# Zero products ahead of the state and join products of a chunked recurrence

## The chip, the cores and the metric

The program runs on one NeuronCore of one Trainium2 chip. The metric is the device time of one execution in microseconds. Of the kernel before there are three timed runs and one profiled execution.

## What is computed

One inference step of two decoder layers for a prompt of 1024 tokens and eight samples. Layer 0 is a convolution branch beside a sparse-attention branch. Layer 1 is RWKV-7 time mixing, and only this layer's recurrence is touched. For each of 16 heads with a 64 x 64 state S it is, token by token:

```
sa = S kk_t
S  = S * w_t - sa (kk_t * a_t)^T + v_t k_t^T
y_t = S r_t
```

Before it stand the projections r, k, v, z and two small hidden layers for w and a, behind it a norm over each head, a gate and an output projection.

## The kernel before

`phase_d` computes layer 1. The recurrence is done in chunks of 64 tokens. A **unit** is a pair (g, d): 128 tokens (two chunks c = 0, 1) of half of the heads, so there are 16 units. Four generators serve a unit:

- `s1` loads the unit's rows and makes its factors, with products into `sm` and `pa` (L1361 to L1431);
- `s2` inverts small triangular blocks on VectorE;
- `joinUT` joins the blocks into the 64 x 64 inverse `UT`. It has four join steps, each a burst of tiny products into the one bank `pg`: L1488 and L1496 with 64 products each, L1511 and L1519 with 16 each. A first step writes `pg`, ScalarE copies it to `Gs` (L1490), the second step multiplies `Gs` into a new `pg`, that is copied into `UT`, and the last two steps do the same again (copies L1514 and L1522);
- `s3` carries the state. Per chunk it multiplies the state into half 0 of the bank `pA` (the first state step, `pA<-SV,AM`, L1541), copies this to `E` on VectorE (L1549), multiplies `UT` by `E` into half 1 of `pA` (the second state step, `pA<-E,UT`), copies it to `SV` (L1560, L1561), and accumulates the new state and the outputs in `pB`.

Beside the units runs the **background**: the projections of the second half of the prompt, z, and the output projections (`t_proj`, `t_sigma`, `t_a`, `t_out`), with products of 256 or 512 columns (L1195 to L1197, L1245 to L1248, L1807 to L1809). The list `F1` holds it. For every unit the loop makes eight turns; a turn takes one step of `s3`, in turns 4 to 7 one join step of the next unit, a step of `s2` of the next unit, one of `s1` of the unit after it, and then about one step of the background.

That loop is the order in which the instructions are traced. The order on each engine's queue is set by a scheduler that simulates the program: what it takes to be ready goes first, and what is traced earlier has precedence. So a state product can be queued ahead of background that was traced before it. An instruction given to `keep_in_program_order` is queued behind the instruction of its engine that was traced last before it. TensorE takes its queue's products in order.

In the last unit (7, 1) `warm` already puts four zero products into a `pg` bank behind each of the six steps of `s3` (L1531), 24 in all.

The `pg`, `pA` and `pB` banks exist once each.

Of the kernel before, what the change touches and what calls it, by code (L numbers as in the profile page):

```python
# [10 lines left out]
BF = mybir.dt.bfloat16  # L11
# [1098 lines left out]
def phase_d(nc, tc, I, O, G):  # L1110
# [4 lines left out]
    flat = lambda t: t.rearrange("p a b -> p (a b)")  # L1115
    with ExitStack() as es:
# [3 lines left out]
        late = pool("dl", 1)  # L1120
# [321 lines left out]
        def s2(g, d, J):  # L1442
# [31 lines left out]
                nc.sync.dma_start(UT[16 * b:16 * b + 16, :, o:o + 16], ud[b * 8:b * 8 + 8].rearrange("c s t -> s c t"))  # L1474
            yield

        def joinUT(J):
            UT = J.UT
            ABf = J.AB.rearrange("p j c t -> p (j c) t")
            U = up.tile([128, 2, 8, 32], F32, name="U")  # L1480
            for o in range(2):
                nc.vector.transpose(U[:, o], UT[:, :, 32 * o:32 * o + 32])
            pg = pq.tile([128, 8, 32], F32, name="pg")
            Gs = up.tile([128, 8, 32], F32, name="Gs")
            for c in range(8):
                for a in range(0, 128, 32):
                    o = a // 32 % 2
                    nc.tensor.matmul(pg[a:a + 32, c, 0:16], lhsT=ABf[a:a + 16, c, 32 * o:32 * o + 32],  # L1488
                                     rhs=U[a:a + 16, o, c, 0:16], start=True, stop=True)
            nc.scalar.activation(Gs[:, :, 0:16], pg[:, :, 0:16], AF.Copy)  # L1490
            yield
            pt = pq.tile([128, 8, 32], F32, name="pg")
            for c in range(8):
                for a in range(0, 128, 32):
                    o = a % 64
                    nc.tensor.matmul(pt[a:a + 16, c, 0:16], lhsT=Gs[a:a + 32, c, 0:16], rhs=UT[a:a + 32, c, o + 16:o + 32],  # L1496
                                     start=True, stop=True)
            for a in range(0, 128, 32):
                o = a % 64 + 16
                if a % 64:  # L1500
                    nc.vector.tensor_copy(UT[a:a + 16, :, o:o + 16], pt[a:a + 16, :, 0:16])
                else:
                    nc.scalar.activation(UT[a:a + 16, :, o:o + 16], pt[a:a + 16, :, 0:16], AF.Copy)
            U = up.tile([128, 8, 32], F32, name="U")
            nc.vector.transpose(U, UT[:, :, 0:32])
            yield
            pg = pq.tile([128, 8, 32], F32, name="pg")
            Gs = up.tile([128, 8, 32], F32, name="Gs")
            for c in range(8):
                for a in (0, 64):  # L1510
                    nc.tensor.matmul(pg[a + 32:a + 64, c, 0:32], lhsT=ABf[a:a + 32, c, 32:64], rhs=U[a:a + 32, c],  # L1511
                                     start=True, stop=True)
            for a in (0, 64):
                nc.scalar.activation(Gs[a + 32:a + 64], pg[a + 32:a + 64, :, 0:32], AF.Copy)  # L1514
            yield
            pt = pq.tile([128, 8, 32], F32, name="pg")
            for c in range(8):
                for a in (0, 64):
                    nc.tensor.matmul(pt[a:a + 32, c, 0:32], lhsT=Gs[a + 32:a + 64, c], rhs=UT[a + 32:a + 64, c, 32:64],  # L1519
                                     start=True, stop=True)  # L1520
            for a in (0, 64):
                nc.vector.tensor_copy(UT[a:a + 32, :, 32:64], pt[a:a + 32, :, 0:32])  # L1522
            yield

        wz = late.tile([128, 512], BF, name="wz")
        nc.gpsimd.memset(wz, 0.0)

        def warm(n):
            z = pq.tile([128, 8, 32], F32, name="pg")
            for _ in range(n):  # L1530
                tc.keep_in_program_order(nc.tensor.matmul(flat(z), lhsT=wz[:, 0:128], rhs=wz[:, 0:256], start=True, stop=True))  # L1531

        def s3(g, d, J):
            wn = 4 if (g, d) == (7, 1) else 0
            AM, SV, MRB, BK, PC, UT = J.AM, J.SV, J.MRB, J.BK, J.PC, J.UT
            js = slice(4 * d, 4 * d + 4)
            for h, i in HV:
                nc.gpsimd.tensor_copy(SV[h, :, i, 0], ST[h, js])
            Y = up.tile([128, 4, 128], F32, name="Y")
            MH = [(m, h, i) for m in range(4) for h, i in HV]  # L1540
            mm = lambda out, lhsT, rhs, start: nc.tensor.matmul(out, lhsT=lhsT, rhs=rhs, start=start, stop=True,  # L1541
                                                                skip_group_check=True)
            for c in range(2):
                pA = py_.tile([128, 2, 4, 64], F32, name="pA")
                pB = py_.tile([128, 2, 4, 64], F32, name="pB")
                for m, h, i in MH:
                    mm(pA[h, 0, m], AM[:, m, i, c], SV[:, m, i, c], m == 0)
                E = up.tile([128, 4, 64], F32, name="E")
                nc.vector.tensor_copy(E, pA[:, 0])  # L1549
                pc = PC.rearrange("p (m c) -> p m c", c=2)[:, :, c]  # L1550
                for m, h, i in MH:
                    mm(pB[h, 1, m], SV[h, m, i, c], AM[h, m, 2, c], m == 0)
                for h, i in HV:
                    mm(pB[h, 0], ident[h, h], SV[h, :, i, c], False)
                if wn:
                    warm(wn)
                yield
                for m, h, i in MH:
                    mm(pA[h, 1, m], UT[h, 2 * m + c], E[h, m], False)
                nc.scalar.activation(SV[0:64, :, 0, c], pA[0:64, 1], AF.Copy)  # L1560
                nc.vector.tensor_copy(SV[64:128, :, 1, c], pA[64:128, 1])  # L1561
                if wn:
                    warm(wn)
                yield
                for m, h, i in MH:
                    mm(pB[h, 0, m], BK[:, m, c, i], SV[:, m, i, c], False)
                for m, h, i in MH:
                    mm(pB[h, 1, m], SV[:, m, i, c], MRB[:, m, c, i], False)
                for h, i in HV:
                    dst = SV[h, :, i, 1] if c == 0 else ST[h, js]  # L1570
                    nc.vector.tensor_tensor(dst, pB[h, 0], pc[h].unsqueeze(2).to_broadcast([64, 4, 64]), op=MUL)
                nc.scalar.activation(Y[:, :, 64 * c:64 * c + 64], pB[:, 1], AF.Copy)
                if wn:
                    warm(wn)
                yield
            yc = (py_ if YC else pm).tile([128, 512], F32, name="pA" if YC else "sm")
            nc.tensor.matmul(yc, lhsT=K["cent"], rhs=flat(Y), start=True, stop=True)
            ycv = yc.rearrange("p (m t) -> p m t", m=4)
            sq = up.tile([128, 4, 128], F32, name="sq")
            nc.scalar.activation(flat(sq), yc, AF.Square)  # L1580
            for m in range(4):
                nc.scalar.activation(Y[:, m], ycv[:, m], AF.Copy, scale=V(4 * d + m, 3))
            yield
            var = (py_ if YC else pm).tile([128, 512], F32, name="pB" if YC else "sm")
            nc.tensor.matmul(var, lhsT=K["bones"], rhs=flat(sq), start=True, stop=True)
            nc.scalar.activation(flat(sq), var, AF.Ln, scale=1.0 / 64, bias=C["eps_gn"])
            nc.scalar.activation(sq, sq, AF.Exp, scale=-0.5)
            nc.vector.tensor_tensor(sq, Y, sq, op=MUL)
            nc.vector.tensor_tensor(sq, sq, J.bv, op=ADD)
            if TL and (g, d) == (7, 1):  # L1590
                G.Y = sq
            else:
                nc.sync.dma_start(YT[g // 2][d][:, :, g % 2 * 128:g % 2 * 128 + 128], sq)
            yield
# [254 lines left out]
        g1 = [s1(*units[u], JJ[u]) for u in range(16)] + [none, none]  # L1849
        g2 = [s2(*units[u], JJ[u]) for u in range(16)] + [none]  # L1850
        gj = [joinUT(J) for J in JJ] + [none]
        for g in (g1[0], g1[1], g2[0], gj[0]):
            for _ in g:
# [32 lines left out]
def body(tc, I, O, stage="all"):  # L1886
# [4 lines left out]
    with ExitStack() as es:  # L1891
# [34 lines left out]
        if stage == "C":  # L1926
            for q in range(2):
                nc.sync.dma_start(O["d_x1T"][:, :, q * 512:q * 512 + 512], G.scr["x1T"][q][:, :, 0:512])
            return
        phase_d(nc, tc, I, O, G)  # L1930


# [80 lines left out]
```

## Time and profile before

| | |
|---|---|
| median of 3 runs | 2153.94 us (2147.12 to 2162.48) |
| profiled execution, its own time | 2146.61 us |
| its span, first to last instruction | 2144.6 us |
| busy: TensorE products, VectorE, ScalarE, GpSimd | 85%, 69%, 53%, 44% |
| mean granted TensorE clock | 0.889 |

A granted clock of 1.00 is TensorE's upper level, 2.4 GHz, and 0.50 its lower, 1.2 GHz. "Busy" of TensorE is the union of its products' durations, whose ends are modelled. An fp32 product appears as two records, so the 8 products of a state step count as x16 in the rows. Idle time before an instruction is that of its engine, with what ended it.

### The profile page before, as it was taken

How to read it: one execution, taken by the hardware profiler on the slowest of the kernel's cores; microseconds unless marked ns; L12 is line 12 of the kernel's file. 1: busy time of each engine (PE TensorE's matmuls, PEld its weight loads, DVE VectorE, ACT ScalarE, POOL GpSimd, SP SyncE). 2: the span in 40 equal slices, each digit the busy share in tenths (PEclk: the TensorE clock that was granted, in tenths of full speed). 3: DMA queues.
4: the chain of work that ended last, by engine and by line, in shares of the span. 5: the costliest groups of instructions: out<-in, count | busy, mean ns of one | idle time of the engine just before them, and what ended most of it. 6: DMA issues, size and time to landing. Idle time of an engine off the chain costs nothing. (4 is left out here: it accounts for less than half of the span.)

```text
span 2144.6 us, 41476 instructions
## 1 busy us (share of the span) xinstructions
PE 1826.6 (85%) x16106; PEld 1528.2 (71%) x16106; DVE 1474.2 (69%) x2550; ACT 1144.5 (53%) x2353; POOL 934.3 (44%) x765
## 2 busy tenths in 40 slices
PE   5997997848998998798878899899999886999875
PEld 5896886836776786575767898678688754976654
DVE  5998995467887788425645347873855899466864
ACT  3233224555665556356746555865874467455544
POOL 4667676564655455354534421242344435212211
PEclk9898998958998887798889899979789997999778
DMA  6424334440221112545656534443443445443443
GB/s 241 140 71 148 119 121 172 170 146 19 68 63 49 53 54 65 165 129 156 184 190 197 173 117 106 130 133 115 126 146 126 146 144 166 131 112 103 152 148 101
DMA packets 231519, 273.18 MB, mean 127 GB/s; under 512 B 71481, under 2 KB 171505, under 8 KB 227162
## 3 DMA queue, kind: packets, MB, share of 16 engines
q1 hardware_dynamic: 210136, 213.11, 32.5%
q0 software_dynamic: 7616, 41.52, 5.8%
q10 hardware_dynamic: 13570, 15.90, 2.1%
q8 instruction: 127, 2.08, 0.4%
q14 instruction: 70, 0.57, 0.1%
HBM read 210.37 MB, written 64.27 MB: 128 GB/s over the span
## 5 line engine op out<-in xcount | busy, mean ns | idle before, releaser
L121 POOL TENSOR_TENSOR wl<-w,wh 128x1024 fp32r<-128x1024 f32 x76 | 195.5, 2573 | 341.6 <-ACT wh L113 330.3
L1195 PE MATMUL mm<-xh,wh 128*128 128x256 f32 (+1 forms) x1024 | 308.2, 303 | 20.9 <-ACT og L1330 10.9
L1197 PE MATMUL mm<-xh,wl 128*128 128x256 f32 (+1 forms) x1024 | 300.5, 295 | 4.4 <-POOL wl L121 4.4
L1196 PE MATMUL mm<-xl,wh 128*128 128x256 f32 (+1 forms) x1024 | 302.8, 296 | 1.6 <-POOL xk L1215 0.8
L1195 PEld LDWEIGHTS mm<-xh,wh 128*128 128x128 f32 x1024 | 202.6, 199 | 33.4 <-ACT og L1330 13.7
L113 ACT ACTIVATE wh<-w 128x1024 fp32r<-128x1024 f32 (+1 forms) x122 | 126.0, 1034 | 165.5 <-DMA w<-in_w_fm 60.7
L1197 PEld LDWEIGHTS mm<-xh,wl 128*128 128x128 f32 x1024 | 202.9, 199 | 9.5 <-POOL wl L121 5.6
L1196 PEld LDWEIGHTS mm<-xl,wh 128*128 128x128 f32 x1024 | 204.3, 200 | 5.1 <-issue 2.1
L268 DVE SCALAR_TENSOR_TENSOR c<-U,cw,c 128x1024 f32<-128x1024 f32 x120 | 198.0, 1674 | 0.9
L604 POOL TENSOR_TENSOR Pl<-PT,Ph 128x512 fp32r<-128x512 f32 (+1 forms) x102 | 132.1, 1299 | 145.9 <-DVE Ph L603 114.9
L252 POOL TENSOR_TENSOR cbuf<-cbuf 128x256 f32<-128x256 f32 (+2 forms) x72 | 131.1, 1827 | 85.8 <-ACT cbuf L250 82.9
L217 PE MATMUL S<-xh,wh 128*128 128x344 f32 (+1 forms) x432 | 147.1, 341 | 23.3 <-ACT wh L113 19.3
L219 PE MATMUL S<-xh,wl 128*128 128x344 f32 (+1 forms) x432 | 145.6, 337 | 14.6 <-POOL wl L121 11.2
L218 PE MATMUL S<-xl,wh 128*128 128x344 f32 (+1 forms) x432 | 146.7, 340 | 3.8 <-POOL xl L121 3.7
L1223 POOL TENSOR_TENSOR xl<-xs,xh 128x520 fp32r<-128x520 f32 (+1 forms) x76 | 106.5, 1404 | 82.5 <-ACT xh L1222 80.7
L250 ACT ACTIVATE cbuf<-cbuf,wrow 128x256 f32<-128x256 f32 x192 | 79.3, 495 | 113.3 <-DMA cbuf<-in_ccmp,cix 72.1
L1219 DVE SCALAR_TENSOR_TENSOR xs<-xk,mu,xs 128x512 f32<-128x512 f32 x96 | 94.4, 989 | 55.2 <-ACT xs L1218 54.3
L217 PEld LDWEIGHTS S<-xh,wh 128*128 128x128 f32 (+1 forms) x432 | 85.4, 198 | 25.6 <-ACT wh L113 24.1
L562 DVE TENSOR_REDUCE nm<-S 128x1 f32<-128x640 f32 (+7 forms) x128 | 88.2, 698 | 19.8 <-PE S L558 19.0
L219 PEld LDWEIGHTS S<-xh,wl 128*128 128x128 f32 (+1 forms) x432 | 84.9, 197 | 19.7 <-POOL wl L121 13.4
L602 ACT ACTIVATE PT<-mm 128x512 f32<-128x512 f32 (+1 forms) x102 | 59.4, 586 | 57.9 <-PE mm L590 46.8
L218 PEld LDWEIGHTS S<-xl,wh 128*128 128x128 f32 (+1 forms) x432 | 84.9, 196 | 7.0 <-POOL xl L121 4.5
(666 smaller groups left out, 5305.1 us busy)
## 6 DMA issues: line engine op xcount, KB each, us to landing
w<-in_w_rkvz SPq DMA_DIRECT2D x64, 512.0 KB
w<-in_w_out SPq DMA_DIRECT2D x32, 512.0 KB
w<-in_w_fm SPq DMA_DIRECT2D x25, 512.0 KB
xk<-x1T SPq DMA_DIRECT2D x48, 260.0 KB
xk<-x1T SPq DMA_DIRECT2D x48, 256.0 KB
w<-in_w_out SPq DMA_DIRECT2D x16, 256.0 KB
x<-in_xp SPq DMA_DIRECT2D x8, 512.0 KB
x<-x ACTq DMA_DIRECT2D x8, 512.0 KB
```

Of the source, the lines that this page charges most:

```text
L113: nc.scalar.activation(hi, src, AF.Copy, **({} if scale is None else {"scale": scale}))
L121: e_lo.tensor_tensor(lo, src, hi, op=SUB)
L217: nc.tensor.matmul(dst, lhsT=wh[:, k, 0:n], rhs=xh[:, k, sl], start=k == 0, stop=False)
L218: nc.tensor.matmul(dst, lhsT=wh[:, k, 0:n], rhs=xl[:, k, sl], start=False, stop=False)
L219: nc.tensor.matmul(dst, lhsT=wl[:, k, 0:n], rhs=xh[:, k, sl], start=False, stop=k == 7)
L252: nc.gpsimd.tensor_tensor(bv[:, 0:n], bv[:, 0:n], bv[:, n:2 * n], op=ADD)
L268: e.scalar_tensor_tensor(c[:, i, 0:T], u[:, k:k + T], cwh[:, i, k:k + 1], c[:, i, 0:T], op0=MUL, op1=ADD)
L604: lambda: nc.gpsimd.tensor_tensor(Pl[:, 0:w], PT[:, 0:w], Ph[:, 0:w], op=SUB)]
L1195: nc.tensor.matmul(dst, lhsT=wh[:, k], rhs=xh[k][:, lo:hi], start=k == 0, stop=False)
L1196: nc.tensor.matmul(dst, lhsT=wh[:, k], rhs=xl[k][:, lo:hi], start=False, stop=False)
L1197: nc.tensor.matmul(dst, lhsT=wl[:, k], rhs=xh[k][:, lo:hi], start=False, stop=k == 7)
L1223: (nc.vector if early[0] and k % LD == 0 else nc.gpsimd).tensor_tensor(lo[k][:, 0:n], t[:, 0:n], hi[k][:, 0:n], op=SUB)
```

## The change

Two functions get zero products of 128 x 128 by 256 bf16 columns, two at a time, each kept in program order. In `joinUT` they are written into the bank of each of the four join steps before its real products, in `s3` into half 0 of `pA` before the first state step and into half 1 before the second, for both chunks, in all 16 units. The real products that follow overwrite them or add to zeros. The zero tile `wz` is made half as wide and is traced earlier.

```
+        wz = late.tile([128, 256], BF, name="wz")
+        nc.gpsimd.memset(wz, 0.0)
+        def fillw(z, n):
+            for _ in range(n):
+                tc.keep_in_program_order(nc.tensor.matmul(z, lhsT=wz[:, 0:128], rhs=wz, start=True, stop=True,
+                                                          skip_group_check=True))
...
             pg = pq.tile([128, 8, 32], F32, name="pg")
+            fillw(flat(pg), 2)
...
             pt = pq.tile([128, 8, 32], F32, name="pg")
+            fillw(flat(pt), 2)
...
-        wz = late.tile([128, 512], BF, name="wz")
-        nc.gpsimd.memset(wz, 0.0)
...
+                fillw(pA[:, 0].rearrange("p m t -> p (m t)"), 2)
                 for m, h, i in MH:
                     mm(pA[h, 0, m], AM[:, m, i, c], SV[:, m, i, c], m == 0)
...
                 yield
+                fillw(pA[:, 1].rearrange("p m t -> p (m t)"), 2)
                 for m, h, i in MH:
                     mm(pA[h, 1, m], UT[h, 2 * m + c], E[h, m], False)
```

The two `pg` pairs shown stand twice, once for the join of 16-blocks and once for that of 32-blocks.

## Rows read from the trace of the kernel before

**Rows 1.** Windows of the unit loop: length, busy (count) per engine, granted clock, DMA.
```profile
1250.00:1360.00 110.00, 102.92 (x1471) 88.09 (x1469) 80.44 (x159) 72.91 (x163) 24.37 (x30) 1.00 0.43 119
1360.00:1440.00 80.00, 68.61 (x783) 51.77 (x784) 69.06 (x137) 64.83 (x132) 28.55 (x35) 0.79 0.43 125
1440.00:1495.00 55.00, 54.34 (x713) 50.03 (x712) 19.75 (x40) 23.55 (x52) 11.47 (x9) 1.00 0.35 107
1495.00:1580.00 85.00, 75.97 (x924) 60.53 (x925) 69.22 (x134) 68.76 (x153) 36.52 (x44) 0.78 0.46 142
1580.00:1690.00 110.00, 106.51 (x1206) 96.04 (x1206) 63.20 (x113) 58.57 (x118) 44.44 (x32) 1.00 0.46 139
...
1830.00:1905.00 75.00, 74.13 (x1021) 65.40 (x1021) 36.11 (x79) 42.98 (x85) 15.04 (x14) 1.00 0.33 97
...
sum 850.00, PE 754.49 PEld 609.67 DVE 600.93 ACT 518.49 POOL 253.69; mean PE 75.45 PEld 60.97 DVE 60.09 ACT 51.85 POOL 25.37
```
**Rows 2.** Windows of the 18 stretches at half clock between 1250 and 2100.
```profile
1362.00:1365.40 3.40, 3.31 (x33) 2.85 (x35) 1.47 (x3) 3.35 (x5) 0.90 (x1) 0.50 0.42 123
...
2082.20:2089.00 6.80, 6.11 (x52) 2.81 (x46) 1.23 (x4) 4.51 (x9) 0.00 (x0) 0.50 0.09 21
sum 173.90, PE 143.54 PEld 109.04 DVE 139.92 ACT 110.81 POOL 57.09; mean PE 7.97 PEld 6.06 DVE 7.77 ACT 6.16 POOL 3.17
```
**Rows 3.** Windows of the 4 us ahead of each of these 18 stretches.
```profile
1395.50:1399.50 4.00, 3.24 (x89) 2.52 (x90) 3.09 (x7) 3.88 (x9) 1.29 (x1) 1.00 0.48 159
...
1740.30:1744.30 4.00, 0.00 (x0) 0.00 (x0) 3.96 (x4) 0.00 (x0) 1.86 (x2) 1.00 0.14 54
...
sum 72.00, PE 33.51 PEld 23.88 DVE 62.82 ACT 43.81 POOL 23.27; mean PE 1.86 PEld 1.33 DVE 3.49 ACT 2.43 POOL 1.29
```
**Rows 4.** TensorE by line, 1250 to 2100: count, busy us, mean ns, idle before, releasers.
```profile
L1195 PE MATMUL mm<-xh,wh 128*128 128x256 f32 (+1 forms) x634 | 188.0, 299 | 2.7 <-DVE og L1327 2.4 <-ACT wh L113 0.3
...
L1541 PE MATMUL pB<-SV,BK 128*64 128x64 f32 x496 | 33.3, 249 | 13.0 <-ACT SV L1560 7.3 <-DVE SV L1561 5.6
L1541 PE MATMUL pA<-SV,AM 128*64 128x64 f32 x512 | 30.8, 244 | 4.7 <-DVE SV L1571 4.5
L1541 PE MATMUL pA<-E,UT 64*64 64x64 f32 x496 | 27.1, 251 | 7.7 <-DVE E L1549 4.1 <-DVE UT L1522 3.4
L1541 PE MATMUL pB<-MRB,SV 128*64 128x64 f32 x496 | 25.7, 241 | 0.0
L1541 PE MATMUL pB<-AM,SV 64*64 64x64 f32 x512 | 24.4, 235 | 2.4 <-ACT sq L1586 2.4
L1541 PE MATMUL pB<-SV,ident 64*64 64x256 f32 x128 | 21.4, 408 | 0.0
...
L1488 PE MATMUL pg<-U,AB 16*32 16x16 f32 x1024 | 18.7, 188 | 6.9 <-DVE U L1482 4.3 <-DVE st L1683 1.9 <-DVE XI L1445 0.7
...
L1496 PE MATMUL pg<-UT,Gs 32*16 32x16 f32 x1024 | 13.4, 177 | 2.2 <-ACT Gs L1490 2.2
L1519 PE MATMUL pg<-UT,Gs 32*32 32x32 f32 x512 | 12.9, 197 | 7.2 <-ACT Gs L1514 7.0
L1511 PE MATMUL pg<-U,AB 32*32 32x32 f32 x512 | 12.5, 195 | 2.8 <-DVE U L1505 2.2 <-ACT og L1330 0.5
```
**Rows 5.** Timeline of TensorE in unit 15: start, duration, product and count.
```profile
2089.78 0.61 PE L1531 MATMUL pg<-wz 128*128 128x256 bf16 x4
2090.32 0.68 PE L1541 MATMUL pA<-E,UT 64*64 64x64 f32 x16
...
2106.11 0.61 PE L1531 MATMUL pg<-wz 128*128 128x256 bf16 x4
2106.48 0.48 PE L1737 MATMUL mm<-wl,xh 128*128 128x512 f32 x1
```
**Rows 6.** Timeline of TensorE in unit 4: a state step and background.
```profile
1497.88 0.68 PE L1541 MATMUL pA<-E,UT 64*64 64x64 f32 x16
...
1523.12 0.28 PE L1248 MATMUL mm<-xh,wh 128*128 128x264 f32 x1
```

More of the change, by code (lines that the diff above doesn't have):

```diff
@@ L1507, in joinUT @@
             pg = pq.tile([128, 8, 32], F32, name="pg")
+            fillw(flat(pg), 2)
             Gs = up.tile([128, 8, 32], F32, name="Gs")
@@ L1516, in joinUT @@
             pt = pq.tile([128, 8, 32], F32, name="pg")
+            fillw(flat(pt), 2)
             for c in range(8):
```

## Prediction

> **What bounds the kernel now.** I read the windows of the unit loop first, because the change touches nothing before it: 850 us from 1250 to 2100, of which TensorE is busy 754.5 and VectorE 600.9 [rows 1]. These means hide two regimes. In four stretches, 350 us together, the clock is at 1.00 and TensorE is busy 102.9 + 54.3 + 106.5 + 74.1 = 337.9 us, or 97%: there TensorE is the bound, it already runs at the upper level, and a product more is time more. In the others the clock is 0.78 or 0.79 and VectorE and ScalarE are as busy as TensorE: in 1360 to 1440 it is 69.1 and 64.8 us beside 68.6, of 80 [rows 1]. There TensorE waits for data.
>
> Then the windows cut at the granted clock. Between 1250 and 2100 it lies at 0.50 in 18 stretches, 173.9 us together; TensorE is busy 143.5 of them and VectorE 139.9, or 80% [rows 2]. Third, the 4 us ahead of each of these falls: TensorE is idle 72.0 - 33.5 = 38.5 us of 72, 2.1 us a fall, while VectorE is busy 62.8, or 87% [rows 3]. So the clock falls after TensorE has waited. Last, the lines of TensorE in the loop tell what it waits for: ahead of the steps that get zero products it is idle 4.7 + 7.7 + 6.9 + 2.2 + 7.2 + 2.8 = 31.5 us in all 16 units, ended by copies on VectorE and ScalarE [rows 4].
>
> **The change, part by part.** *Count.* A unit gets 4 joins and 2 chunks x 2 state steps, two products each: 8 pairs. 16 units make 128 pairs, 256 products. No DMA and no evacuation is added. The zero tile's fill stays one GpSimd operation of half the size, and GpSimd is busy 253.7 of 850 us [rows 1]: nothing.
>
> *Price of a pair.* Four such products at clock 1.00 last 0.61 us to the end of the last; background behind them starts 0.37 us after their start, a state step 0.54 us after it [rows 5]. That is 0.09 to 0.135 each, so a pair costs 0.19 to 0.27 us, and I take 0.22. No zero product runs at 0.50 in the trace; with half the clock I bound it at twice, 0.44.
>
> *Which pairs can hide.* The first state step and the first join step of each two write a bank whose readers are long done, so their pairs can run while the real products still wait. The idle time there is 4.7 + 6.9 + 2.8 = 14.4 us [rows 4]. The second state step writes the other half of the bank that `E` is being copied from, and the second and fourth join steps write the one `pg` bank that `Gs` is being copied from. Their zero products have to wait for those copies, and so do the real ones: this half, 64 pairs, can't fill the wait and lengthens the chain behind it. (Should the halves of `pA` be tracked apart, 32 of these pairs could run early; their idle time is 7.7 us [rows 4].) What queues behind a waiting pair on TensorE is everything, background too, but the real products stood there with the same wait.
>
> *Sum of the pairs.* By time, 350/850 of the 128 pairs, 53, fall into the full stretches: 53 x 0.22 = 11.7 us, with no idle time to hide in (12 us are left in 350). The other 75 fall where TensorE is busy 754.5 - 337.9 = 416.6 of 500 us. If the 83 us of idle time takes all of them the cost is nothing; if each is paid at half clock it is 75 x 0.44 = 33 us. I charge the half that can't run early, 38 x 0.22 = 8.4 us. Together 20 us; ends 12 and 45.
>
> *What the clock gives back.* If every product in the cold stretches ran twice as fast, TensorE would win 143.5/2 = 72 us [rows 2]; if no fall is averted, nothing. A pair against the 2.1 us idle of a mean fall is small. In the fullest of the 18, at 1395.5, only 0.76 us are idle and one or two pairs can change it; at 1740.3 no product was issued in 4 us and no pair can, as it stands in the same queue [rows 3]. I take a sixth of the cold time away: 29 us x (143.5/173.9)/2 = 12 us of TensorE time. VectorE is 80% busy in these stretches and is late next, so I count half: 6 us. The Trainium skill, page "TensorE: Matmul & The Clock Gate", section "Terms", gives the penalty of a cold clock as the throttled time times the missing share of the clock, here 173.9 x 0.5 = 87 us; by that alone the sum would be 20 - 87, 67 us faster. The trace does not support all of it: TensorE stood idle for 30 of these 173.9 us, and a faster clock does not shorten a wait for VectorE [rows 2, 3].
>
> *What is moved.* Each pair is queued behind the TensorE instruction traced last before it, and the real products behind the pair. Today a state step can be queued ahead of background. In unit 4 the second state step runs at 1497.88, while the last product of the hidden layer, which the loop traces in the turn before it, runs at 1523.12, 25 us later [rows 6]. With the change this step goes behind that product; while the background waits for its inputs, the state cannot fill in. A join step in turns 4 to 7 likewise goes behind the state step of its own turn. The price lies in stretches like 1360 to 1440 and 1495 to 1580, 165 us. Upper bound: all state and join products (33.3 + 30.8 + 27.1 + 25.7 + 24.4 + 21.4 + 18.7 + 13.4 + 12.9 + 12.5 = 220 us in 850 [rows 4]) of these stretches run alone and no longer beside waiting background: 220 x 165/850 = 43 us. Below nothing it can go too, since the simulated order is not the best one: at most the 20 us that TensorE is idle in the two stretches [rows 1]. The nearest row is the background's own, which waits only 2.7 us in 634 products [rows 4], so it is mostly ready; I take 2 us.
>
> *Total.* +20 - 6 + 2 = +16 us. On the profiled execution: 2146.6 + 16 = 2162.6. The median of the runs lies 7.3 us above that execution; runs of the changed kernel should too, so **2170 us**, 0.8% above 2153.94. About 1%, 21.5 us, is what can be told from no change here.
>
> **The rivals.**
>
> *A. Slower: the order costs.* Place: units 1 to 6, where the background starts new projections and hidden layers. The state steps wait behind background that waits for its inputs, and TensorE idles where it now alternates. At half of the bound, 21 us, with 20 for the pairs and 3 back: +38, so 2192 us. It decides when the order costs over 8 us more than I took. For it: the 25 us lead of [rows 6]. Against it: the 2.7 us [rows 4].
>
> *B. Faster: the clock holds.* The pairs keep the clock up where the tiny join and state products let it fall. If nine tenths of the 72 us come back and the pairs cost 20, it is -45: 2109 us. It needs over 42 us back to be faster by 1%. For it: 18 falls, and after several of them long stretches with many small products (the cold stretches hold all kinds of steps). Against it: the idle time ahead of the falls [rows 3] and VectorE's 80% [rows 2]. The skill's rule cited above is this rival's.
>
> *C. It does not do what it says.* The scheduler queues other products between a pair and its real step, or the pair waits as long as the step. Then the clock gets nothing and the 20 us are paid, in part hidden: +12 to +20, 2166 to 2174 us. Nothing in the trace shows which; the 64 pairs behind the same copy speak for it.
>
> **How the numbers follow.** My forecast 0.33, C 0.11, both within 1%: same 0.44. A and worse 0.39, as the unknown order is an open term on that side. B 0.17. The range: below, part of B, with 35 us of clock and only 12 us of pairs, 2154 - 23 = 2131; above, A with the whole 43 us of order, 20 for the pairs and 5 back, 2154 + 58 = 2212. Outside it lie the strongest cases of B and prices of 45 us for the pairs together with a bad order, about 0.2.
>
> **What would show it.** Right, if L1531's kin, the new line, has 256 products at about 110 ns from start to start in warm stretches, if the windows at 1.00 grow by some 0.22 us a pair, and if the 18 falls stay about as many with idle time ahead of them. The order's price shows as more idle time ahead of the new products, ended by copies or by background's inputs, and as state steps no longer ahead of background. Wrong on the fast side, if the mean clock of the loop rises from 0.90 (173.9 of 850 us at half [rows 1, 2]) to 0.95 or more and the span shrinks with it; wrong on the slow side, if TensorE's idle time in the loop grows well beyond today's 95.5 us [rows 1].

## The result, and the profile after

The changed kernel takes **2239.53 us**, median of 4 runs (2227.95 to 2244.10), beside 2150.53 for the kernel before (4 runs): a ratio of 1.0401 [1.036, 1.0442], 89 us slower. I had forecast 2170 and a range up to 2212, so forecast and range are both wrong. The side is that of rival A, but A's price was 2192.

The profiled execution has a span of 2242.3 us. The window of its loop, as in [rows 1] (length, busy and count of TensorE, weight load, VectorE, ScalarE and GpSimd, granted clock, DMA share, GB/s):

```profile
1250.00:2197.70 947.70, 817.46 (x9736) 649.52 (x9735) 608.63 (x1181) 533.04 (x1097) 263.75 (x246) 0.87 0.40 122
```

The loop grew from 850 to 947.7 us, by 97.7. TensorE's busy time grew by 63.0 us (754.5 before), its idle time by 34.7 (95.5 to 130.2). VectorE's work grew by only 8 us.

The stretches of this loop at half clock, as in [rows 2]; there are 24 where there were 18, and the last line is their sum:

```profile
2168.80:2179.00 10.20, 4.95 (x14) 3.58 (x12) 3.16 (x10) 1.24 (x4) 0.00 (x0) 0.50 0.22 64
...
sum 245.80, PE 208.59 PEld 162.15 DVE 182.60 ACT 154.23 POOL 74.95; mean PE 8.69 PEld 6.76 DVE 7.61 ACT 6.43 POOL 3.12
```

The falls were not averted; half-clock time rose by 72 us, and TensorE's work in it by 65.1. At half clock that added work takes 32.5 us more than at full clock. The 97.7 us are thus 34.7 of idle time, 32.5 of slow clock, and 30.5 of more work.

The lines of TensorE in the loop, as in [rows 4] (line, product, count | busy us, mean ns | idle time just before, by what ended it). L1482 holds the new products, L1550 the state products, L1497 the first join step (32 products of two records each in a unit):

```profile
L1195 PE MATMUL mm<-xh,wh 128*128 128x256 f32 (+1 forms) x655 | 198.9, 304 | 9.6 <-DVE og L1327 5.3 <-ACT wh L113 3.3 <-ACT xh L1222 1.0
...
L1407 PE MATMUL pa<-AM,KBK 64*128 64x128 f32 x512 | 67.0, 345 | 27.3 <-DVE KBK L1386 11.2 <-DVE KBK L1385 7.7 <-DVE MRB L1413 5.1
...
L1550 PE MATMUL pB<-SV,BK 128*64 128x64 f32 x480 | 29.5, 243 | 15.1 <-DVE SV L1572 10.2 <-ACT SV L1571 4.8
L1482 PE MATMUL pg<-wz 128*128 128x256 bf16 x128 | 27.2, 298 | 6.2 <-DVE UT L1511 3.5 <-ACT Gs L1525 2.8
...
L1482 PE MATMUL pA<-wz 128*128 128x256 bf16 x124 | 25.9, 293 | 1.2 <-DVE E L1559 1.1
L1550 PE MATMUL pA<-SV,AM 128*64 128x64 f32 x496 | 25.9, 241 | 5.9 <-DVE SV L1582 5.6
L1550 PE MATMUL pA<-E,UT 64*64 64x64 f32 x490 | 23.9, 242 | 0.2 <-DVE UT L1534 0.2
...
L1497 PE MATMUL pg<-U,AB 16*32 16x16 f32 x1024 | 13.2, 188 | 2.7 <-DVE U L1490 2.7
```

The reader is to see two things. All 256 products are there (124 of the 128 in `pA` lie in this window). And the waits have moved. Ahead of the steps named in the prediction, with their pairs, TensorE is idle 6.2 + 1.2 + 5.9 + 0.2 + 2.8 (all four join steps) = 16.3 us, where it was 31.5. Ahead of the second state step 7.7 us became 0.2, and 1.2 ahead of its pair, which now meets the wait first; the first state step waits as before (4.7, now 5.9). Idle time has grown in front of the units' next work and of the background: 27.3 us before L1407 (13.5 in the kernel before), 9.6 before L1195 (2.7).

How late a state step can now run, the timelines show (start, duration, engine, line, product; in brackets the idle time before it). In unit 4, VectorE's copy of `E` and then TensorE:

```profile
1512.27 0.42 DVE L1559 COPY E<-pA 128x256 f32<-128x256 f32 x1
```

```profile
1513.61 0.80 PE L1245 MATMUL mm<-xh,wh 128*128 128x256 f32 x2 [2.99 <-ACT xh L1222]
...
1534.07 0.42 PE L1248 MATMUL mm<-xh,wh 128*128 128x264 f32 x1
1534.30 0.65 PE L1482 MATMUL pA<-wz 128*128 128x256 bf16 x2
1534.88 1.12 PE L1550 MATMUL pA<-E,UT 64*64 64x64 f32 x16
```

`E` is done at 1512.69, and the state step starts at 1534.88, 22.2 us later, right behind the hidden layer's last product. In [rows 6] it ran 25 us ahead of that product, 1.5 us behind its copy, whose line in the kernel before is:

```profile
1496.00 0.42 DVE L1549 COPY E<-pA 128x256 f32<-128x256 f32 x1
```

Unit 15, the last, shows the same at the end of the program, where no other unit's work can make up for it; VectorE's copy, then TensorE:

```profile
2169.14 0.42 DVE L1559 COPY E<-pA 128x256 f32<-128x256 f32 x1
```

```profile
2165.41 0.60 PE L1550 MATMUL pB<-SV,ident 64*64 64x256 f32 x4
2168.44 0.76 PE L1540 MATMUL pg<-wz 128*128 128x256 bf16 x4 [2.43 <-DVE UT L1534]
2174.45 0.80 PE L1747 MATMUL sm<-wh,xh 128*128 128x512 f32 x1 [5.25 <-ACT xh L113]
...
2199.13 0.39 PE L1749 MATMUL mm<-MRB,xl 128*128 128x512 f32 x1
2199.36 0.39 PE L1482 MATMUL pA<-wz 128*128 128x256 bf16 x2
2199.68 0.68 PE L1550 MATMUL pA<-E,UT 64*64 64x64 f32 x16
```

Here `E` was done at 2169.56 and the state step starts 30.1 us later; in [rows 5] the same step, at 2090.32, came 1.2 us behind it. TensorE meanwhile stood idle 5.25 us for the output projection's input. From the first `pB<-AM,SV` product of unit 15 to the end of the span it is 77.4 us; it was 56.0.

These two are the extremes. None of the other 30 second state steps starts more than 11 us behind its copy in the changed kernel, and over all 32 the lateness adds up to 126 us, against 135 before (of which 40 in unit 0 and 25 in unit 9). So the lateness of this step explains unit 4 and unit 15, and not by itself the whole loss.

### The profile page after: what moved, and what is told of

It reads as the page before. It is cut to its first block, busy times and chain, and to the rows that moved or that the text cites. A ratio compares the mean times of both kernels' runs of the same rounds, so it can differ in the third digit from the quotient of the medians.

```text
span 2242.3 us, 41944 instructions
## 1 busy us (share of the span) xinstructions
PE 1884.5 (84%) x16362; PEld 1562.2 (70%) x16362; DVE 1489.2 (66%) x2550; ACT 1150.7 (51%) x2355; POOL 931.8 (42%) x765
## 5 line engine op out<-in xcount | busy, mean ns | idle before, releaser
L1195 PE MATMUL mm<-xh,wh 128*128 128x256 f32 (+1 forms) x1024 | 313.9, 307 | 26.8 <-ACT og L1330 10.6
L1197 PE MATMUL mm<-xh,wl 128*128 128x256 f32 (+1 forms) x1024 | 303.4, 297 | 3.3 <-POOL wl L121 3.3
L1195 PEld LDWEIGHTS mm<-xh,wh 128*128 128x128 f32 x1024 | 206.9, 203 | 42.1 <-ACT og L1330 13.4
L1197 PEld LDWEIGHTS mm<-xh,wl 128*128 128x128 f32 x1024 | 206.5, 202 | 7.0 <-POOL wl L121 4.2
L1407 PE MATMUL pa<-AM,KBK 64*128 64x128 f32 x512 | 67.0, 345 | 27.3 <-DVE KBK L1386 11.2
```

Source lines behind the costliest of these rows:

```text
L1195: nc.tensor.matmul(dst, lhsT=wh[:, k], rhs=xh[k][:, lo:hi], start=k == 0, stop=False)
L1197: nc.tensor.matmul(dst, lhsT=wl[:, k], rhs=xh[k][:, lo:hi], start=False, stop=k == 7)
```

## The experiments

Two theories stood at the start. **Order**: keeping the zero products in program order drags the real steps behind other work. **Products**: the zero products cost more TensorE time than I charged. All ratios are to the kernel before, with 95% intervals; differences in us are between medians.

**The two parts by themselves.** `e1_pins` has no zero products; the first real product of each join and state step is kept in program order instead, and the step's others follow it:

```
+    put = pinned()   # 1st: tc.keep_in_program_order(nc.tensor.matmul(...)); others: add_manual_dep on it
-    mm(pA[h, 0, m], AM[:, m, i, c], SV[:, m, i, c], m == 0)
+    put(pA[h, 0, m], lhsT=AM[:, m, i, c], rhs=SV[:, m, i, c], start=m == 0, ...)
```

> No zero products; instead the first real product of every join step and of both state steps is queued behind the TensorE instruction traced before it, and the other products of the step behind that first one. So this is the change's order without its products. Theory O (the order costs): 40 to 70 us slower than before, 2190 to 2220 us, with TensorE's idle time in the loop well above the 95.5 us of before. Rival P (the products cost, by their time, their wait for the bank or the clock): within 15 us of before, 2135 to 2165 us.

Measured 1.0247 [1.0206, 1.0289], 2202.99 us: **+52**. `e2_free` has all zero products and no fixed place:

```
-    tc.keep_in_program_order(nc.tensor.matmul(z, lhsT=wz[:, 0:128], ...))
+    nc.tensor.matmul(z, lhsT=wz[:, 0:128], ...)
```

> The 256 zero products without being kept in program order; the bank alone ties them to their step. Theory O: the products' own price and little else, 128 pairs at 0.22 us, 15 to 30 us slower than before, 2165 to 2180 us. Rival P: as slow as the changed kernel, 2220 to 2245 us.

Measured 1.0146 [1.0109, 1.0182], 2184.42 us: **+34**. That is 4 us above what the order theory had for it. Both theories hold in part, and 52 + 34 = 86 of the 89 us. The loops of the two as windows, each followed by the sum over its stretches at half clock (18 and 22 of them); `e1_pins`:

```profile
1250.00:2152.40 902.40, 777.66 (x9420) 627.93 (x9419) 611.87 (x1180) 530.76 (x1094) 262.89 (x245) 0.87 0.42 127
```

```profile
sum 238.90, PE 196.94 PEld 152.22 DVE 180.40 ACT 156.61 POOL 77.44; mean PE 10.94 PEld 8.46 DVE 10.02 ACT 8.70 POOL 4.30
```

`e2_free`:

```profile
1250.00:2138.20 888.20, 801.88 (x9811) 634.75 (x9810) 606.39 (x1181) 525.76 (x1091) 258.64 (x242) 0.90 0.42 127
```

```profile
sum 177.40, PE 154.41 PEld 113.21 DVE 129.92 ACT 116.34 POOL 55.19; mean PE 7.02 PEld 5.15 DVE 5.91 ACT 5.29 POOL 2.51
```

Beside [rows 1, 2], order alone adds 29.2 us of idle time (95.5 to 124.7) and 23.2 of busy time for the same products: they run slower, since 53.4 us more of TensorE's work lie at half clock, and half of that, 26.7, is close to the 23.2. The products alone leave the half-clock time where it was (173.9 to 177.4), add 47.4 us of busy time, and fill 9.2 us of idle time.

**Which steps.** `e3_join_only` keeps the four `fillw` calls of `joinUT`, `e4_state_only` the two of `s3`.

> Zero products, kept in program order, ahead of the four join steps only. Theory O, with the state steps held behind background as the main price: 20 to 45 us slower, 2170 to 2195 us. Rival P: half of the products, so half of the loss, about 45 us, 2195 us; both halves would then add up to the whole.

Measured 1.018 [1.0141, 1.0218], 2187.11 us: +37.

> Zero products, kept in program order, ahead of the two state steps only. Theory O: the larger part of the loss, 45 to 75 us slower, 2195 to 2225 us. Rival P: half of the loss, about 45 us, 2195 us.

Measured 1.0309 [1.0272, 1.0346], 2215.48 us: +65. The state steps carry most. The two sum to 4.9%, more than the 4.0% of the whole; that in part they delay the same chain would fit, and isn't shown.

**Where the order costs.** `e5_pins_last` pins only the state steps of unit 15, `e6_pins_butlast` everything except them:

```
e5:  put = pinned() if (g, d) == (7, 1) else nc.tensor.matmul    # joins: nc.tensor.matmul
e6:  put = pinned() if (g, d) != (7, 1) else nc.tensor.matmul    # joins: pinned()
```

> No zero products; only the state steps of unit 15 are queued behind the instruction traced before them. Theory L (in the last unit the second state step gets stuck behind the last output projection, which is traced before it and waits for weights): 15 to 22 us slower than before, 2165 to 2173 us. Rival E (the order's 53 us are spread evenly over the units): 3 us, 2150 to 2157 us.

Measured 1.011 [1.0069, 1.0152], 2173.60 us: **+23** for four steps of one unit.

> No zero products; join and state steps queued behind the instruction traced before them, as in e1_pins, but not the state steps of unit 15. Theory L: the rest of the order's loss, 30 to 38 us slower than before, 2180 to 2189 us. Rival E: 15/16 of it, 50 us, 2200 us.

Measured 1.0169 [1.0138, 1.02], 2186.42 us: **+36**. Together 59 against 52, within the intervals. In the traces, unit 15's last part is 73.8 us long in e5 and 58.5 in e6 (56.0 before, 75.4 in e1), so 18 us of e5's price arise there; its trace is 8 us late before that part begins, 5 of them already at unit 0, where nothing is changed. The unit in which e5's price arises, seen in e1 (TensorE; L1558 and L1484 are state products, L1757 the output projection):

```profile
2122.20 0.60 PE L1558 MATMUL pB<-SV,ident 64*64 64x256 f32 x4
...
2131.52 0.80 PE L1755 MATMUL sm<-wh,xh 128*128 128x512 f32 x1 [7.58 <-ACT xh L113]
...
2155.12 0.39 PE L1757 MATMUL mm<-MRB,xl 128*128 128x512 f32 x1
2155.44 0.68 PE L1484 MATMUL pA<-E,UT 64*64 64x64 f32 x16
```

It is the picture of the changed kernel with none of the change's zero products in it.

`e11_pins_early` pins the units up to 6 (joins up to 7), `e14_state_early` only the state steps of units up to 6:

```
e11: put = pinned() if J.u <= 7 else nc.tensor.matmul    # joins; state steps: J.u <= 6
e14: put = nc.tensor.matmul                              # joins; state steps: pinned() if J.u <= 6
```

> No zero products; join and state steps queued behind the instruction traced before them in units 0 to 6 alone (the joins of units 0 to 7). Theory T (the order costs where the background changes from one projection to the next, up to unit 6, and at the end): all of e6_pins_butlast's 36 us, 2180 to 2190 us. Rival E (spread evenly): 7/15 of it, 17 us, 2163 to 2170 us.

Measured 1.0169 [1.012, 1.0219], 2189.68 us: +35. All of e6's price lies in these units.

> No zero products; only the state steps of units 0 to 6 are queued behind the instruction traced before them, the joins are free. Theory T (state held behind background where the projections change): most of e11_pins_early's 36 us, 22 to 36 us slower than before. Rival J (the joins behind the state steps cost as much): 10 to 20 us.

Measured 1.0106 [1.0024, 1.0188], 2181.01 us: +28. The interval, 5 to 40 us, holds both theories' ranges, so how the price is split between state steps and joins isn't shown.

Against the kernel before, unit starts in e1 are 38 us late at unit 5, 10 at unit 6, 31 at unit 7, then 20 to 39, and 33 at unit 15. So of the 40 us lost in unit 4, where the state step is late, 28 are made up in unit 5, which has less background left to do, and unit 6 costs 21 that stay (21 in e6, e11 and e14 too). There TensorE is only 3 us more idle, but 34 us of the unit are at half clock and none were before. Its middle, in the kernel before and in e1:

```profile
1640.00:1660.00 20.00, 20.00 (x262) 17.27 (x262) 15.15 (x28) 12.44 (x26) 7.27 (x7) 1.00 0.30 94
```

```profile
1660.00:1670.00 10.00, 10.00 (x45) 7.96 (x44) 4.07 (x9) 3.08 (x8) 0.00 (x0) 0.50 0.23 52
```

Which wait or which order of products lets the clock fall in that unit isn't shown.

**The price of a product, and the clock.** The number per place is changed to one, to four, and to four without a fixed place:

```
-    fillw(flat(pg), 2)
+    fillw(flat(pg), 1)      # e7_one;  e8_four and e9_free4: 4, e9 without keep_in_program_order
```

> The changed kernel with one zero product at each place instead of two, 128 in all. Theory F (a burst costs a fixed 0.21 us behind its last product, plus 0.11 us for each product): 128 x 0.11 = 14 us faster than the changed kernel, 2225 us. Rival N (the price goes with the number of products): half of the products' 33 to 41 us, 2218 to 2223 us.

Measured 1.0383 [1.0328, 1.0437], 2234.90 us. Both theories had it lower; it is 5 us below the changed kernel, less than the two intervals can tell apart.

> The changed kernel with four zero products at each place, 512 in all. Theory F: 256 more at 0.11 us, 28 us slower than the changed kernel, 2265 us, or less where they keep the clock up. Rival N: twice the products' 33 to 41 us, 2272 to 2280 us. A rival C, the clock: with twice the products the half-clock time of the loop, 245 us, falls below 200 us and the time comes out under 2245 us.

Measured 1.0427 [1.0396, 1.0458], 2242.67 us, as rival C had it.

> Four zero products at each place, not kept in program order (e2_free has two). Theory F (a burst of n costs 0.21 + 0.11 (n - 1) us at full clock): 256 more products at 0.11 us, 28 us, less what the clock gives back. In e8_four the half-clock time of the loop fell from 245 to 174 us and nearly paid for the same 28 us. With the same return: 2180 to 2195 us. Rival C (with a free order the clock pays more than the price): half-clock time under 110 us and under 2170 us. Rival D (the clock gives nothing here, since the order's stalls are what four products bridged): half-clock time still about 175 us, 2205 to 2220 us.

Measured 1.023 [1.0175, 1.0285], 2205.15 us: +50, rival D's time.

None (e1_pins), one, two and four products per place give 1.0247, 1.0383, 1.0401 and 1.0427: the first adds some 29 us, the next three together 10. Bursts at full clock, from the first product's start to the state step's (timelines of TensorE: `e7_one`, the changed kernel, `e8_four`):

```profile
2152.76 0.28 PE L1482 MATMUL pA<-wz 128*128 128x256 bf16 x1
2152.98 0.69 PE L1550 MATMUL pA<-SV,AM 128*64 128x64 f32 x16
```

```profile
1649.30 0.39 PE L1482 MATMUL pA<-wz 128*128 128x256 bf16 x2
1649.62 0.69 PE L1550 MATMUL pA<-SV,AM 128*64 128x64 f32 x16
```

```profile
1680.56 0.60 PE L1482 MATMUL pA<-wz 128*128 128x256 bf16 x4
1681.09 0.69 PE L1550 MATMUL pA<-SV,AM 128*64 128x64 f32 x16
```

The medians over such bursts (82, 91 and 97) are 0.213, 0.322 and 0.540 us: the first product with the hand-over to the step costs 0.21, each further one 0.11. At half clock a pair takes 0.539 (15 bursts). 128 pairs at 0.322 are 41 us; `e2_free`'s 47.4 us of busy time are these 41 and 5 for the 10.9 us more work at half clock. The changed kernel's 30.5 us of more work are less, 0.24 a pair. The hand-over isn't the zero products' own: in the kernel before, a state or join product comes 0.211 us behind a background product of 256 columns (L1195 to L1197, median of 61, full clock), where background follows background at 0.120. A pair put between the two starts 0.123 behind the background product, so it adds 0.123 + 0.322 - 0.211 = 0.23.

With four products the clock moves. The half-clock sums of `e8_four` and of `e9_free4`:

```profile
sum 174.00, PE 144.39 PEld 106.59 DVE 133.79 ACT 105.23 POOL 47.81; mean PE 6.28 PEld 4.63 DVE 5.82 ACT 4.58 POOL 2.08
```

```profile
sum 160.50, PE 152.78 PEld 114.31 DVE 122.11 ACT 105.15 POOL 49.06; mean PE 7.28 PEld 5.44 DVE 5.81 ACT 5.01 POOL 2.34
```

In these traces of the pinned order, half-clock time falls from 245.8 to 174.0 us and TensorE's work in it by 64.2, worth 32 us; the two more products cost 128 x (0.540 - 0.322) = 28. So the two nearly cancel, as the ratios say. In those of the free order TensorE's work at half clock hardly changes (154.4 to 152.8), and +34 became +50.

One execution is a small sample, though: the 55 runs of the kernel before that stand beside the experiments have clocks from 0.878 to 0.897. An estimate of half-clock time that uses every run is 2 x (1 - clock) x span, over the whole program. Its mean of four runs is 548 us for the changed kernel and 506 for `e8_four`, 492 for `e2_free` and 448 for `e9_free4`, and the runs of one kernel scatter by 9 to 20 (standard deviation). By that, four products save some 42 to 44 us of half-clock time in either order. Why this pays for them in one order and less so in the other isn't shown.

**Controls.** `e10_nowarm` leaves out the zero products that the kernel before already has; `e15_wz` is the kernel before with `wz` moved and halved.

> The kernel before without the 24 zero products that it already has in unit 15, so with none in this loop. Theory F: they stand in a stretch where TensorE waits, so they cost little and give little, within 5 us of before. Rival C (zero products hold the clock at the end, where the chain of waits is the bound): 5 to 15 us slower than before.

Measured 0.999 [0.9964, 1.0016]: those products do nothing that can be measured.

> Only the move and the halving of the zero tile, no product and no order added. Every theory: within 8 us of before.

Measured 1.0002 [0.9962, 1.0041]: the tile costs nothing.

**The opposite order.** If late steps cost 52 us, perhaps earlier ones gain. `e12_prio_state` gives the state turn priority, `e13_prio_both` also the joins:

```
-    step(main)
+    with tc.high_priority(offset=300):
+        step(main)                        # e13 also around step(gj[u + 1])
```

> The kernel before with the opposite of the change's order: the instructions of s3 get the precedence of instructions traced 300 earlier, some three turns of the loop, so that a ready state step goes ahead of background. No zero products are added. Theory O (a state step's place relative to the background sets the time): 5 to 25 us faster than before, 2130 to 2150 us. Rival S (the state already goes ahead whenever it is ready and only holding it back costs): within 10 us of before.

Measured 1.023 [1.0185, 1.0274], 2197.98 us.

> As e12_prio_state, and the join steps get the same precedence too. Theory O: another 0 to 10 us faster than e12_prio_state. Rival S: within 10 us of before.

Measured 1.0691 [1.0649, 1.0733], 2297.37 us. Both are slower, and no theory had said so. In e12's trace the second state step came 13 to 46 us behind its copy in units 3 to 9 and 11 to 14 (at most 11 in the kernel before, but for 25 in unit 9), and in each it started within 5 us of the last copy into the join's `UT`, which it needs. That the priority held back what makes `UT` is only argued.

In e13's trace the loop is 143.5 us longer, with only 8 us more idle time. Half-clock time is 314.0 us, and TensorE's work in it 289.0, 145 more than before, worth 73 us. The remaining 63 are the same products taking longer, and the trace shows a new picture: state and join products one by one between background products:

```profile
1645.63 0.33 PE L1541 MATMUL pA<-SV,AM 128*64 128x64 f32 x2
1645.89 0.39 PE L1196 MATMUL mm<-xl,wh 128*128 128x256 f32 x1
1646.21 0.33 PE L1541 MATMUL pA<-SV,AM 128*64 128x64 f32 x2
1646.46 0.39 PE L1197 MATMUL mm<-xh,wl 128*128 128x256 f32 x1
```

A background product and a state product's two records take 0.57 us here, with two hand-overs. In the loop TensorE changes 702 times between state or join products and other work, 390 times before. That these hand-overs make the 63 us isn't tested. The clock falls here with TensorE at work, too: in 8 of the 32 falls it is busy through all of the 4 us ahead (by the modelled ends), as at 1650.8:

```profile
1646.80:1650.80 4.00, 4.00 (x23) 2.71 (x22) 0.42 (x1) 0.16 (x2) 2.25 (x1) 1.00 0.33 94
```

No version beat the kernel before.

## Why the prediction was wrong, step by step

- **"What is moved ... I take 2 us" failed most.** It measured 52: in e1's trace 29 of idle time and 23 of slower clock. I had the lost lead of the state step: [rows 6] shows the 25 us, and the step lost it. The slower clock I had not in this term at all. And for the size I chose between 43 and -20 by the wrong row: the 2.7 us that background waits in [rows 4]. That is the wait under an order that lets state steps run in its gaps, and says nothing of the gaps once they can't. The row that was near was [rows 6] itself.
- **The upper bound of 43 us was no bound.** It counted units 1 to 6 only, and there it holds (36 and 35 measured in e6 and e11), but by luck: it was made of state and join products that run alone, while in e6's trace TensorE is only 17 us more idle and its work at half clock, 66 us more, takes 33 longer. Unit 15 was not in it: there the state step goes behind the output projection, and the chain behind it ends the program, 23 us in e5. The same comparison as in [rows 6], made for the last unit, would have shown it. I had also read "In the others the clock is 0.78 or 0.79" from two stretches; the others have 0.93, 1.00, 0.56 and 0.84, and the last of them, with unit 15 in it, is the longest:

```profile
1905.00:2100.00 195.00, 164.29 (x1986) 114.35 (x1987) 134.10 (x283) 97.09 (x206) 35.51 (x30) 0.84 0.42 133
```

- **"A pair costs 0.19 to 0.27 us" was too low for the burst itself: 0.32**, and 0.54 at half clock, where my bound was 0.44. [rows 5] had the answer. Four products took 0.54 us to the next state step, which I divided by four. A burst has a fixed part, and one length alone can't show it. Where that hand-over stood before, the pair adds 0.23, as I took it; the loop's added work is 0.33 a pair in `e2_free` and 0.24 in the changed kernel. The products' term, 20 us, measured 34 (23 to 39).
- **"I charge the half that can't run early" was about right where order is free.** I had hidden 37 pairs, 8 us; `e2_free` filled 9.2 us of idle time. As I had it, no pair ahead of a second state step starts before the copy of `E` has ended (0.05 us behind it at the least). In the changed kernel no idle time is seen to be filled: its idle time is 5.5 us above that of `e1_pins`.
- **"What the clock gives back", 6 us, failed too.** Two products gave nothing back that a trace can show in either order (173.9 to 177.4, and 238.9 to 245.8), and the change as a whole lost 32.5 us to the clock. What I saw in [rows 3], that a pair is small beside the idle time ahead of a fall, held. I had not asked what the order does to the clock: it brought 65 us more at half clock, 23 to 27 of the 52 us. More idle time in all isn't the reason by itself: in e14's trace half-clock time is 269.5 us with 6 us more idle time than before. The Trainium skill, page "TensorE: Matmul & The Clock Gate", section "Terms", charges throttled time times the missing share of the clock: by that an estimate for order alone of (238.9 - 173.9) x 0.5 = 33 us. Busy time grew by 23.2, as TensorE is idle in part of those stretches, so here the rule is an upper end.
- **The total.** In place of +20 - 6 + 2 stand 34 for the products with what they hide and 52 for the order.
- **The rivals.** A named the right mechanism, and unit 4's step behaves as it said, but it priced half of a bound that lacked unit 15. B is refuted at two products. C applies in part: at 109 of the 128 places the real step follows its pair directly, and at 19 other work of TensorE comes between, for up to 9 us. 16 of these stand ahead of a step that writes a bank with no copy to wait for, where I had the pair run early. The count, some 110 ns from product to product, the falls with idle time ahead of them (2.4 us in the 4 us ahead of a mean fall), and the free tile came out as written. The falls were to stay about as many, and are 24.

**Open:** why an order with state and joins ahead is slower too. A late step costs, and so does a forced early one, so the order before lies between the two; whether e13's hand-overs are its price wasn't tried. Nor is it shown which part of the early units' 36 us comes from joins alone, as e14's interval is wide, nor why unit 6 runs at half clock once state steps and joins are pinned.

## What to carry to other kernels

An instruction that is fixed in program order brings the whole step behind it along: price the lead that the step had in the trace, unit by unit and in the last unit first, since nothing makes up for a delay there. A burst of filler products has a hand-over as well as a price per product, so read it from its start to the next real product, at two lengths, and see whether a hand-over stood there before. Read the clock from every run and not from one trace. And split such a change before explaining it: order without products and products without order took two runs and gave 86 of the 89 us.

## What the runs showed of the hardware

- A burst of 128 x 128 products by 256 bf16 columns ahead of a 16-product step takes 0.21 us for the first, hand-over included, and 0.11 for each further one, at full clock; a pair at half clock takes 0.54.
- A small state or join product also comes 0.211 us behind a background product of 256 columns with no zero product between, where the next background product comes at 0.120.
- Two such products per step left half-clock time where it was (173.9 to 177.4 us, 238.9 to 245.8). Four cut it by 72 us in the traces of the pinned order and by 17 in those of the free order; by the mean clock of four runs each, an estimate, by 42 and 44.
- In e13, with state and join products singly between background products, the clock fell 8 times of 32 with TensorE busy through the 4 us ahead.
- The 24 zero products that the kernel before had made no difference (0.999 [0.9964, 1.0016]).
